# A hybrid decoder step on one core: a third staging tile, p copies in rows' tiles, reloads into settled places, and gates first in the last pair

## The chip, the cores and the metric

The kernel runs on one core of one Trainium2 chip. The metric is the device time of one execution in microseconds, as the median of several runs. Beside it there is one profiled execution, from which all rows below are taken.

## The reference

A decoder trunk with one layer of each of two mixers, run for 1024 prompt tokens and 8 sample tokens with shared weights (W = 384, 384 and 264 columns: two blocks of prompt tokens, and a third with the last 256 and the 8 samples).

```python
for i in range(2):
    hn = rmsnorm(h, norm_mix[i])
    if i == 0:   # HGRN2: q, f, i, z = split(hn @ w_in_a); 8 heads, dk 128, dv 256
        y, S = hgrn2_mixer(hn, s_hgrn[j], ...)      # S_t = diag(f_t) S_(t-1) + k_t v_t^T, o_t = S_t^T q_t
                                                    # y = (rmsnorm(o) * silu(z)) @ w_out
    else:        # gated MLP: u, v, z = split(hn @ w_in_b), u = gelu(u), v = layernorm(gelu(v))
        s = einsum('gts,bnsgd->bntgd', w_spatial, v) + b_spatial   # 8 groups, chunks of 128 tokens
        y = (u * s * silu(z)) @ w_out
    h = h + y
    gate = sigmoid(rmsnorm(h, norm_ple[i]) @ w_ple_gate[i])
    h = h + gate * (p[i] @ w_ple_proj[i])
y = rmsnorm(h, norm_final)
```

It returns the outputs for prompt and samples, the HGRN2 states of both, and the normalised v rows of the last chunk.

## The kernel before

Everything lies with features on the partitions and tokens in the columns, in the three column blocks c = 0, 1, 2. A product in full precision is three matmuls on high and low halves (`mm3`, L213 to L215: hi x hi, lo x hi, hi x lo). A weight tile is fetched into `wstg`, cast to its high half `whi` by ScalarE (L145), and VectorE subtracts that to get the low half `wlo` (L146). Activations are split the same way (L208, L209). `tc.high_priority(offset=PRI)` lets a scheduler put the instructions inside it earlier in their engine's order; otherwise they stand about as the code is written, and each engine works through its own order. SyncE issues all the transfers, in its order too.

**Heads.** Eight heads of layer 0 run one after the other, as several generators that are advanced in turns by ticks. In a head, `q` and `k` are multiplied by decay factors level by level (L644, L645), `k` is then transposed on TensorE (`pt_k`, L660). The gate path `zs` (L541) uses sigmoids in a ring of two tiles `sg`. In the last head (h = 7) the same ring also holds the p input of layer 0 (`p_in_act(0, ...)`, L334), which is fetched and split there. `out_sum` (L671, L672) copies a head's output and sums its squares.

**Units.** Layer 1's three input products are done in units of 2x2 blocks with seven products instead of eight (`unit`): weight tiles `a[0]` and `a[1]` of a unit are fetched (`load_unit`, L178), GpSimd makes sums of their quarters (`ssum`, L182 to L189), and ScalarE and VectorE split these (`shi`, `slo`) and the plain ones. In `unit`, VectorE adds the products up in `u2`, `u4` and `c22`; the sum `c` (L1121) reads the bank `ps_d`, which a later product writes again. For each group g from 0 to 7 there is a gated unit (for u, with a gelu) and then a spatial unit (for z): in it TensorE multiplies the v rows by `w_spatial` (`psp`, L1206), VectorE scales that and adds `bt` (`s`, L1208), GpSimd multiplies by u (L1214), ScalarE takes the sigmoid of z (L1219), VectorE multiplies twice (L1220, L1221), and SyncE stores the result to `ozd` (L1222). All `wstg` tiles come from one ring of two.

**The last pair.** While group 7's spatial unit runs, the stored results are fetched again for the output projection: `load_zt`/`zq` makes 20 transfers of 128x384 into a ring of five tiles `zq` (L346), each split by ScalarE (L350) and VectorE (L353). Behind the unit comes the second half of p's product, `pple(1, ph, pl, 1, ...)`: 12 groups `ps_pple`, each copied by ScalarE to `pple_t` (L329) in a ring of four tiles and stored to `ppd` (L330). `ps_pple` has three banks. Then come the products of the output projection (`ps_o`).

**Norms.** `norm_sum` adds a constant to the column sums `pss` (L268, and L270 for the block c = 2, which has 8 columns more), GpSimd takes the power -1/2 (L222), TensorE spreads it over the partitions (`pbc`, L278).

Of the kernel before, what the change touches and what calls it, by code (L numbers as in the profile page):

```python
# [7 lines left out]
F32 = mybir.dt.float32  # L8
# [71 lines left out]
def trunk_kernel(ctx, tc, xT, st, pT, nrm, wina, lbl, gna, wouta, winb, lng, lnb, lngr, lnbr,  # L80
# [59 lines left out]
    ws = [None]  # L140
# [32 lines left out]
    def load_unit(m):  # L173


        a = [wp.tile([P, 1024], F32, name="wstg") for _ in range(2)]
# [74 lines left out]
    def norm_sum(sp, ssq, c):  # L251

        nt = NT[c]
        cols = nt + (c == 2)
        pss = pp.tile([P, 512], F32, name="pss", tag="po", bufs=1)
        e = sp.tile([P, 3], F32, name="rms_e", bufs=2)
        if c == 2:
            V.memset(e, 1.0)
# [10 lines left out]
        if c == 2:  # L269
            V.tensor_scalar(e[:NS, 2:3], pss[:NS, 2:3], D * EPS, None, ALU.add)  # L270
        return rsqrt(sp, e, 3)

    def norm_bc(y, c):

        pbc = p2[0].tile([P, 512], F32, name="pbc", tag="p2", bufs=2)
        for i in range(NT[c] + (c == 2)):
            n = min(P, W[c] - i * P)
            PE.matmul(pbc[:, i * P:i * P + n], y[:n, i:i + 1].broadcast_to([n, P]), ident[:n, :n], start=True, stop=True)  # L278
# [58 lines left out]
    def load_zt(zt, parts, stage, n=2, lag=0, tie=True):  # L337
# [4 lines left out]
        for i in range(len(todo) + lag):  # L342
            if i < len(todo):
                c, k0, k = todo[i]
                stg.append(stage(W[c]))
                last["zt"] = nc.sync.dma_start(stg[i], ozd[c][:, k0 + k:k0 + k + n, :])  # L346
            if i >= lag:
# [5 lines left out]
                V.tensor_tensor(zl[:, k:k + n, :], stg[i - lag], zh[:, k:k + n, :].bitcast(F32), ALU.subtract)  # L353
            yield
# [67 lines left out]
    fill = pple(0, ph, pl, 0, [(sp, "pple_t", 9)] * 9 + [(fq, "q", 3)] * 3)  # L422
# [82 lines left out]
    def head_proj(h, r):  # L505
# [873 lines left out]
```

## Time and profile before

| | |
|---|---|
| median of 3 runs | 1933.78 us (1931.57 to 1937.53) |
| profiled execution | 1936.32 us, span of its core 1934.6 us |
| mean granted TensorE clock | 0.991 of full speed |
| TensorE busy | 1887.6 us, 13250 matmuls |
| VectorE, ScalarE, GpSimd busy | 1162.3, 800.0, 429.5 us |

A row of a timeline gives the start, the duration, the engine (PE = TensorE, DVE = VectorE, ACT = ScalarE, POOL = GpSimd, SP = SyncE; SPq is SyncE's queue), the line of the kernel, the operation, the tile written and the tiles read, and in brackets the idle time before it with what ended it. Several equal instructions in a row are one row with xN. A wait's row gives the engine and what it stood for, the sum in us, how often, and the longest. Clock shares are of 2.4 GHz; the lower level is 1.2 GHz.

### The profile page before, as it was taken

To read this page: it belongs to the slowest core of one execution; us is meant where nothing else is said; L and a number is where in the kernel's file an instruction comes from. 1 tells how busy PE (TensorE), PEld (TensorE's weight loads), DVE (VectorE), ACT (ScalarE), POOL (GpSimd) and SP (SyncE) were. 2 spreads that over 40 slices of the span, in tenths; PEclk is the share of its full clock that TensorE was granted. 3 is DMA by queue.
4 is the path that set the end of the run, shared out by engine and by line. 5 is a ranking of instruction groups with operands and counts; after the bars stand their busy time and mean duration, and the time that the engine had idled before them with its cause. 6 is when DMAs were issued, how large, how long until landed. Compare 5 with 4: busy or idle time off the path is not lost.

```text
span 1934.6 us, 33674 instructions
## 1 busy us (share of the span) xinstructions
PE 1887.6 (98%) x13250; PEld 1857.7 (96%) x13250; DVE 1162.3 (60%) x2610; ACT 800.0 (41%) x1701; POOL 429.5 (22%) x441
## 2 busy tenths in 40 slices
PE   9999999999999999999999999999999998999997
PEld 8999999999999998999999999999999997999997
DVE  5967776776767676311555655586677776311455
ACT  6453535445454536311344544433343335211242
POOL 4110001001000100011333322344444441011221
PEclk8999999999999999999999999999999999999999
DMA  6232322222231327611244333333323236611123
GB/s 211 75 117 70 110 72 96 78 80 97 72 110 51 109 71 228 215 44 44 94 138 138 98 123 97 96 105 108 96 96 100 100 109 212 191 53 44 66 88 110
DMA packets 123887, 203.75 MB, mean 105 GB/s; under 512 B 11409, under 2 KB 96593, under 8 KB 122705
## 3 DMA queue, kind: packets, MB, share of 16 engines
q1 hardware_dynamic: 123728, 201.61, 32.2%
q8 instruction: 104, 1.70, 0.4%
q14 instruction: 55, 0.44, 0.1%
HBM read 148.75 MB, written 52.82 MB: 104 GB/s over the span
## 4 chain that ended last, share of the span: by engine, by line
PE 78%; DVE 10%; DMA 4%; issue 3%; POOL 2%; ACT 2%; SPq 0%; DVEq 0%; POOLq 0%; ACTq 0%
PE ps_proj L213 15%; PE ps_proj L214 15%; PE ps_proj L215 15%; PE ps_o L213 6%; PE ps_o L214 6%; PE ps_o L215 6%; DVE wlo L146 1%; DMA vn<-vraw 1%; PE ps_d L213 1%; PE ps_d L215 1%; PE ps_d L214 1%; PE pC L642 1%; PE pt_o L683 1%; DMA wstg<-in_winb 1%; PE p L608 1%
## 5 line engine op out<-in xcount | busy, mean ns | idle before, releaser
L213 PE MATMUL ps_proj<-bh,whi 128*128 128x384 f32 (+1 forms) x2160 | 695.8, 322 | 4.0 <-DVE zs L541 2.4
L214 PE MATMUL ps_proj<-bl,whi 128*128 128x384 f32 (+1 forms) x2160 | 679.2, 314 | 1.2 <-POOL bl L209 1.2
L215 PE MATMUL ps_proj<-bh,wlo 128*128 128x384 f32 (+1 forms) x2160 | 679.9, 315 | 0.2 <-DVE wlo L146 0.2
L213 PEld LDWEIGHTS ps_proj<-bh,whi 128*128 128x128 f32 x2160 | 407.8, 189 | 5.7 <-DVE zs L541 3.0
L214 PEld LDWEIGHTS ps_proj<-bl,whi 128*128 128x128 f32 x2160 | 408.2, 189 | 2.3 <-POOL bl L209 2.3
L215 PEld LDWEIGHTS ps_proj<-bh,wlo 128*128 128x128 f32 x2160 | 406.8, 188 | 0.8 <-DVE wlo L146 0.8
L146 DVE TENSOR_TENSOR wlo<-wstg,whi 128x1024 fp32r<-128x1024 f32 x148 | 190.3, 1285 | 129.1 <-ACT whi L145 128.3
L145 ACT CAST whi<-wstg 128x1024 fp32r<-128x1024 f32 x148 | 155.2, 1049 | 129.1 <-PE ps_proj L214 72.9
L249 POOL TENSOR_TENSOR ssq<-ssq,tmp 128x384 f32<-128x384 f32 (+1 forms) x72 | 76.2, 1058 | 407.1 <-ACT tmp L248 360.3
L862 DVE TENSOR_TENSOR h<-h,ps_o 128x384 f32<-128x384 f32 (+1 forms) x48 | 24.6, 512 | 193.8 <-PE ps_o L215 188.4
L248 ACT ACTIVATE tmp<-h 128x384 f32<-128x384 f32 (+1 forms) x72 | 35.3, 491 | 219.2 <-DVE h L862 168.8
L145 ACT CAST shi<-ssum 128x512 fp32r<-128x512 f32 x88 | 53.9, 621 | 172.1 <-POOL ssum L182 97.4
L213 PE MATMUL ps_o<-bh,whi 128*128 128x384 f32 (+1 forms) x384 | 122.1, 318 | 0.0
L214 PE MATMUL ps_o<-bl,whi 128*128 128x384 f32 (+1 forms) x384 | 121.8, 317 | 0.0
L215 PE MATMUL ps_o<-bh,wlo 128*128 128x384 f32 (+1 forms) x384 | 121.8, 317 | 0.0
L146 DVE TENSOR_TENSOR slo<-ssum,shi 128x512 fp32r<-128x512 f32 x88 | 73.7, 839 | 51.5 <-ACT shi L145 51.5
L213 PE MATMUL ps_o<-zh,whi 128*128 128x384 f32 (+1 forms) x288 | 90.1, 313 | 0.0
L215 PE MATMUL ps_o<-zh,wlo 128*128 128x384 f32 (+1 forms) x288 | 89.7, 312 | 0.0
L214 PE MATMUL ps_o<-zl,whi 128*128 128x384 f32 (+1 forms) x288 | 89.7, 312 | 0.0
L209 POOL TENSOR_TENSOR ql<-q,qh 128x384 fp32r<-128x384 f32 (+1 forms) x24 | 22.7, 947 | 234.1 <-ACT qh L208 218.8
L214 PEld LDWEIGHTS ps_o<-bl,whi 128*128 128x128 f32 x384 | 72.2, 188 | 0.0
L213 PEld LDWEIGHTS ps_o<-bh,whi 128*128 128x128 f32 x384 | 72.2, 188 | 0.0
(283 smaller groups left out, 3901.3 us busy)
## 6 DMA issues: line engine op xcount, KB each, us to landing
wstg<-in_wina SPq DMA_DIRECT2D x48, 512.0 KB, 3.6
wstg<-in_winb SPq DMA_DIRECT2D x48, 512.0 KB, 4.0
zstg<-ozd SPq DMA_DIRECT2D x22, 384.0 KB, 3.9
pj<-ppd SPq DMA_DIRECT2D x16, 516.0 KB, 4.0
S<-in_st SPq DMA_DIRECT2D x16, 512.0 KB, 4.8
vb<-vd SPq DMA_DIRECT2D x16, 512.0 KB, 5.0
out_so_s<-S SPq DMA_DIRECT2D x16, 512.0 KB, 3.3
wstg<-in_wouta SPq DMA_DIRECT2D x16, 512.0 KB, 3.7
```

What stands on the lines that cost most here:

```text
L145: A.copy(hi, src)
L146: V.tensor_tensor(lo, src, hi.bitcast(F32), ALU.subtract)
L209: last["lo"] = eng.tensor_tensor(lo, src, hi.bitcast(F32), ALU.subtract)
L213: PE.matmul(ps, wh, xh, start=first, stop=False, skip_group_check=more)
L214: PE.matmul(ps, wh, xl, start=False, stop=False, skip_group_check=more)
L215: PE.matmul(ps, wl, xh, start=False, stop=last, skip_group_check=more)
L248: A.activation(sq[:, :w], src, AF.Square)
L249: eng.tensor_tensor(ssq, ssq, sq[:, :w], ALU.add)
L608: PE.matmul(blk(p0, i), blk(Y, i), blk(X, i), start=True, stop=True)
L642: PE.matmul(pC[b:b + l, o + l:o + 2 * l], kb, qb, start=True, stop=True)
L683: PE.transpose(pt[:, m, :], on[:, m * P:(m + 1) * P], ident)
L862: V.tensor_tensor(hr[c][m], hr[c][m], ps[:, :W[c]], ALU.add)
```

## The change

- **Third staging tile.** Every third allocation of `load_unit` takes a tile `wstg3` of its own, so a unit's second weight tile reuses the first one of the unit before.
- **Spatial units.** The operation `s` (L1208, now L1231) has high priority in all of them. In group 7 the sigmoid and both products have it as well.
- **Reloads.** The 20 reloads of the last pair go to five places that the last spatial unit's first operations have finished with (`rw` twice, `bspb` twice, `gb`), and each next one is fetched behind a split instead of ahead of it.
- **p copies.** The last half of p's product is copied into the 12 tiles `hr[c][4 + mm]`, which later hold rows of h, instead of a ring of four.
- **Last head.** p of layer 0 goes through the ring `vf` instead of `sg`; the decay products of q and k and the operations of `out_sum` have high priority there. In all heads, `sample` has two ticks more ahead of each update of its state and fewer behind them.
- **Norms.** All sums `pss` fill 128 rows, so one operation adds the constant for every block, and no memset is needed.

```diff
 def load_unit(m):
-    a = [wp.tile([P, 1024], F32, name="wstg") for _ in range(2)]
+    a = []
+    for _ in range(2):
+        a.append(ws[0].tile([P, 1024], F32, name="wstg3", bufs=1) if nst[0] % 3 == 2 else
+                 wp.tile([P, 1024], F32, name="wstg"))
+        nst[0] += 1
...
 def norm_sum(sp, ssq, c):
         for i in range(cols):
-            n = min(P, W[c] - i * P)
+            o = min(i * P, W[c] - P)
             for j, t in enumerate(parts):
-                PE.matmul(pss[:n, i:i + 1], t[:, i * P:i * P + n], ones[:, 0:1],
+                PE.matmul(pss[:, i:i + 1], t[:, o:o + P], ones[:, 0:1],
                           start=j == 0, stop=j == len(parts) - 1)
-        V.tensor_scalar(e[:, :nt], pss[:, :nt], D * EPS, None, ALU.add)
-        if c == 2:
-            V.tensor_scalar(e[:NS, 2:3], pss[:NS, 2:3], D * EPS, None, ALU.add)
+        e = sp.tile([P, 3], F32, name="rms_e", bufs=2)
+        V.tensor_scalar(e, pss[:, :3], D * EPS, None, ALU.add)
...
 pple:
-                pl_, tag, bufs = stg[n % len(stg)]
-                n += 1
-                t = pl_.tile([P, 384], F32, name="pple_t", tag=tag, bufs=bufs)
+                t = place(c, mm)
...
 load_zt:
+            if not lag:
+                fetch(i)
             if i >= lag:
                 ...
+            if lag:
+                fetch(i)
...
-                    r["p"] = p_in_act(0, lambda w: fq.tile([P, 384], F32, name="sg", bufs=2)[:, :w])
+                    r["p"] = p_in_act(0, lambda w: wa.tile([P, 384], F32, name="vf", bufs=2)[:, :w])
...
-            V.tensor_tensor(ql[:, :, 1, :], ql[:, :, 1, :], t2[:, :, 0:1].broadcast_to([P, n, lv]), ALU.mult)
-            V.tensor_tensor(kl[:, :, 0, :], kl[:, :, 0, :], t2[:, :, 1:2].broadcast_to([P, n, lv]), ALU.mult)
+            with tc.high_priority(offset=PRI if h == NH - 1 else 0):
+                V.tensor_tensor(ql[:, :, 1, :], ql[:, :, 1, :], t2[:, :, 0:1].broadcast_to([P, n, lv]), ALU.mult)
+                V.tensor_tensor(kl[:, :, 0, :], kl[:, :, 0, :], t2[:, :, 1:2].broadcast_to([P, n, lv]), ALU.mult)
...
 out_sum:
+        with tc.high_priority(offset=PRI if last_head[0] else 0):
...
 sample:
             nc.sync.dma_start(vb, ...)
+            yield 2
...
-        yield 10
+        yield 6
...
 spatial, pre():
+            with tc.high_priority(offset=PRI):
                 V.scalar_tensor_tensor(s[:, :nt * P]..., pss[:, :nt, :], lg[:, 0, m:m + 1], bts[mm]..., ...)
 spatial, out():
+            with tc.high_priority(offset=PRI if g == 7 else 0):
                 A.activation(sg[:, :w], src, AF.Sigmoid)
                 V.tensor_tensor(sg[:, :w], sg[:, :w], src, ALU.mult)
                 V.tensor_tensor(s[:, :w], s[:, :w], sg[:, :w], ALU.mult)
...
+            zq_to = itertools.cycle([t[:, 3 * i:3 * i + 3, :].rearrange("p a b -> p (a b)") for t in (rw, bspb)
+                                     for i in range(2)] + [gb.rearrange("p a b -> p (a b)")[:, :384]])
             zq = load_zt(zt, [(1, 0), (0, 0), (1, 4), (1, 8)],
-                         lambda w: wb2.tile([P, 384], F32, name="zq", bufs=ZQ)[:, :w].rearrange(...),
+                         lambda w: next(zq_to)[:, :w].rearrange("p (k t) -> p k t", k=1),
                          1, ZQ, False)
...
-              ..., pple(1, ph, pl, 1, [(sp, "tmp", 4)]))
+              ..., pple(1, ph, pl, 1, lambda c, mm: hr[c][4 + mm]))
```

GpSimd's order at a spatial unit and the gated unit behind it, before (L1214 are the products `s` by u, L182 and L187 the first two sums of the gated unit, L1243 and L1244 the normalised rows of the last chunk):

```order
L1214 TENSOR_TENSOR s<-s,u 128x264
L189 TENSOR_TENSOR ssum<-wstg,ssum 128x512
L1214 TENSOR_TENSOR s<-s,u 128x384 x3
L1213 COPY s<-ss__14932 128x8
L1214 TENSOR_TENSOR s<-s,u 128x264
L182 TENSOR_TENSOR ssum<-wstg 128x512
L187 TENSOR_TENSOR ssum<-wstg 128x512
L1243 TENSOR_TENSOR gb<-vn,gb 128x256
L1244 TENSOR_TENSOR gb<-gb 128x256
L184 TENSOR_TENSOR ssum<-ssum,wstg 128x512
L189 TENSOR_TENSOR ssum<-wstg,ssum 128x512
```

and of the change, where L1237 are these products and L188 and L193 these sums:

```order
L1237 TENSOR_TENSOR s<-s,u 128x384
L195 TENSOR_TENSOR ssum<-wstg,ssum 128x512
L1237 TENSOR_TENSOR s<-s,u 128x384
L188 TENSOR_TENSOR ssum<-wstg 128x512
L193 TENSOR_TENSOR ssum<-wstg 128x512
L1237 TENSOR_TENSOR s<-s,u 128x384
L1236 COPY s<-ss__14926 128x8
L1237 TENSOR_TENSOR s<-s,u 128x264
L190 TENSOR_TENSOR ssum<-ssum,wstg 128x512
L1267 TENSOR_TENSOR gb<-vn,gb 128x256
L1268 TENSOR_TENSOR gb<-gb 128x256
L195 TENSOR_TENSOR ssum<-wstg,ssum 128x512
```

The two sums that stood behind the last product `s` now stand ahead of the last two products of the spatial unit.

ScalarE's order at the end of the last spatial unit, before (L1219 the sigmoids, L350 the casts of reloads, L329 the copies of p's product):

```order
L350 CAST xmh_11627<-zq 128x384
L145 CAST whi<-wstg 128x1024
L350 CAST xmh_11627<-zq 128x384 x2
L1219 ACTIVATE sg<-u_18599 128x384
L350 CAST xmh_11627<-zq 128x384
L329 COPY pple_t<-ps_pple 128x384 x3
L350 CAST zh_0_18852<-zstg 128x528
L329 COPY pple_t<-ps_pple 128x384
L350 CAST zh_0_18852<-zstg 128x528
```

and of the change (L1243 the sigmoids, L363 the casts, L338 the copies):

```order
L363 CAST xmh_11621<-bspb 128x384
L146 CAST whi<-wstg 128x1024
L1243 ACTIVATE sg<-u_18588 128x384
L363 CAST xmh_11621<-rw 128x384
L363 CAST xmh_11625<-rw 128x384
L363 CAST xmh_11625<-bspb 128x384 x2
L363 CAST xmh_11625<-gb 128x384
L338 COPY h_4_18786<-ps_pple 128x384
L338 COPY h_5_18787<-ps_pple 128x384
L338 COPY h_6_18788<-ps_pple 128x384
L363 CAST zh_0_18826<-zstg 128x528
L338 COPY h_7_18789<-ps_pple 128x384
```

Five casts of reloads now stand between the last sigmoid and the first copy, where one stood. VectorE's order at the same place, of the change (L1155 the last sum of the unit, L1244 and L1245 the products behind a sigmoid, L366 the low halves of reloads):

```order
L366 TENSOR_TENSOR bl_11636<-rw,bh_11633 128x384
L1245 TENSOR_TENSOR s<-s,sg 128x384
L1155 TENSOR_TENSOR u_18588<-ps_d,u_18588 128x384
L366 TENSOR_TENSOR xml_11622<-bspb,xmh_11621 128x384 x2
L1244 TENSOR_TENSOR sg<-sg,u_18588 128x384
L366 TENSOR_TENSOR xml_11622<-gb,xmh_11621 128x384
L1245 TENSOR_TENSOR s<-s,sg 128x384
L366 TENSOR_TENSOR xml_11622<-rw,xmh_11621 128x384
L366 TENSOR_TENSOR xml_11626<-rw,xmh_11625 128x384
L147 TENSOR_TENSOR wlo<-wstg,whi 128x1024
L366 TENSOR_TENSOR xml_11626<-bspb,xmh_11625 128x384 x2
L366 TENSOR_TENSOR xml_11626<-gb,xmh_11625 128x384
```

The low half of the reload in `gb` now stands behind the product of the last sigmoid, and the low halves of the last five reloads behind that.

VectorE's order in the last head, before (L644 and L645 the decay products, L541 the gate path `zs`, L146 the low half of a weight tile):

```order
L541 SCALAR_TENSOR_TENSOR zs_9299<-ps_proj,gn_707,sg 128x384
L209 TENSOR_TENSOR Sl<-S,Sh 128x256
L209 TENSOR_TENSOR bl_125<-sg,bh_122 128x264
L353 TENSOR_TENSOR bl_123<-zstg,bh_120 128x768
L644 TENSOR_TENSOR q<-q,t_9557 128x2x64
L146 TENSOR_TENSOR wlo<-wstg,whi 128x1024
L645 TENSOR_TENSOR k<-k,t_9557 128x2x64
L650 TENSOR_TENSOR asum<-Am_712,pC 128x256
L541 SCALAR_TENSOR_TENSOR zs_9300<-ps_proj,gn_707,sg 128x384
L708 SCALAR_TENSOR_TENSOR S<-S,t_9427,pd 128x256
L209 TENSOR_TENSOR al<-asum,ah 128x256
```

and of the change (L661 and L662 the decay products, L557 `zs`, L147 the low half):

```order
L366 TENSOR_TENSOR bl_123<-zstg,bh_120 128x768
L557 SCALAR_TENSOR_TENSOR zs_9297<-ps_proj,gn_705,sg 128x384
L661 TENSOR_TENSOR q<-q,t_9546 128x2x64
L662 TENSOR_TENSOR k<-k,t_9546 128x2x64
L728 SCALAR_TENSOR_TENSOR S<-S,t_9405,pd 128x256
L667 TENSOR_TENSOR asum<-Am_710,pC 128x256
L366 TENSOR_TENSOR bl_123<-zstg,bh_120 128x768
L215 TENSOR_TENSOR Sl<-S,Sh 128x256
L366 TENSOR_TENSOR bl_123<-zstg,bh_120 128x768
L147 TENSOR_TENSOR wlo<-wstg,whi 128x1024
L215 TENSOR_TENSOR al<-asum,ah 128x256
```

The product for `k` stood behind the low half `wlo`; now it and `q` stand ahead of it, and `al` stands behind it.

## Rows read from the trace of the kernel before

**Rows 1.** the page's busy time, share of the span and instructions of each engine

```profile
PE 1887.6 (98%) x13250; PEld 1857.7 (96%) x13250; DVE 1162.3 (60%) x2610; ACT 800.0 (41%) x1701; POOL 429.5 (22%) x441
```

**Rows 2.** TensorE's waits, whole span: us in total, times, longest us

```profile
PE ps_d L213 <- DVE c L1121: 8.6, 7, 2.4
PE ps_pple L213 <- ACT pple_t L329: 7.9, 4, 5.4
PE pt_k L660 <- DVE k L645: 3.1, 1, 3.1
PE ps_proj L213 <- DVE zs L541: 2.4, 2, 1.7
PE psp L1206 <- DVE s L1208: 1.2, 1, 1.2
```

**Rows 3.** windows: length, busy us (instructions) of each engine, granted clock, DMA share, GB/s

```profile
745.00:755.00 10.00, 8.00 (x53) 7.17 (x54) 8.03 (x14) 6.85 (x18) 1.87 (x2) 0.83 0.59 176
1310.00:1320.00 10.00, 7.61 (x41) 7.29 (x40) 4.67 (x7) 3.33 (x6) 3.68 (x4) 0.83 0.30 92
1360.00:1370.00 10.00, 8.08 (x46) 8.07 (x46) 4.43 (x7) 4.62 (x8) 1.90 (x3) 0.83 0.30 81
1637.50:1645.00 7.50, 7.41 (x38) 7.41 (x39) 3.17 (x4) 5.60 (x12) 0.00 (x0) 0.70 0.96 329
```

**Rows 4.** all engines' waits in the units, 1255 to 1600 us

```profile
POOL ssum L182 <- DMA wstg<-in_winb: 102.8, 12, 11.3
DVE slo L146 <- ACT shi L145: 29.7, 16, 2.9
```

**Rows 5.** timeline of SyncE and VectorE about one gated unit: start us, us, instruction

```profile
1336.61 0.33 SPq L178 DMA_DIRECT2D wstg<-in_winb  x1
1347.97 0.33 SPq L178 DMA_DIRECT2D wstg<-in_winb  x1
...
1360.72 0.69 DVE L146 TENSOR_TENSOR slo<-ssum,shi 128x512 fp32r<-128x512 f32 x1 [2.06 <-ACT shi L145]
1361.33 0.55 DVE L1121 TENSOR_TENSOR c<-ps_d,u 128x384 f32<-128x384 f32 x1
```

**Rows 6.** timeline of VectorE and GpSimd in the spatial unit before it

```profile
1328.33 1.11 DVE L146 TENSOR_TENSOR slo<-ssum,shi 128x512 fp32r<-128x512 f32 x1 [2.27 <-ACT shi L145]
1340.31 0.68 DVE L146 TENSOR_TENSOR slo<-ssum,shi 128x512 fp32r<-128x512 f32 x1
1345.65 0.56 DVE L1221 TENSOR_TENSOR s<-s,sg 128x384 f32<-128x384 f32 x1
...
1341.59 1.26 POOL L1214 TENSOR_TENSOR s<-s,u 128x384 f32<-128x384 f32 x1 [2.29 <-DVE s L1208]
```

**Rows 7.** DMA issues in the units: KB each, median us from issue to landing

```profile
wstg<-in_winb SPq DMA_DIRECT2D x28, 512.0 KB, 3.7
zq<-ozd SPq DMA_DIRECT2D x5, 192.0 KB, 3.3
```

**Rows 8.** timeline of TensorE, ScalarE and VectorE at the last pair

```profile
1626.46 0.45 PE L213 MATMUL ps_pple<-bh,whi 128*128 128x384 f32 x1 [1.27 <-ACT pple_t L329]
1637.59 0.69 PE L213 MATMUL ps_pple<-bh,whi 128*128 128x384 f32 x1 [5.38 <-ACT pple_t L329]
1643.50 0.28 PE L215 MATMUL ps_pple<-bh,wlo 128*128 128x264 f32 x1
...
1625.54 0.49 ACT L350 CAST xmh<-zq 128x384 fp32r<-128x384 f32 x1
1637.06 0.48 ACT L329 COPY pple_t<-ps_pple 128x384 f32<-128x384 f32 x1 [5.67 <-DMA ppd<-pple_t]
...
1623.70 0.55 DVE L1133 TENSOR_TENSOR u<-ps_d,u 128x384 f32<-128x384 f32 x1
```

**Rows 9.** timeline of ScalarE and VectorE in the last head

```profile
738.81 0.83 ACT L208 CAST bh<-sg 128x384 fp32r<-128x384 f32 x2 [2.89 <-DMA sg<-in_pT]
...
746.13 0.82 DVE L645 TENSOR_TENSOR k<-k,t 128x128 f32<-128x128 f32 x1
```

More of the change, by code (lines that the diff above doesn't have):

```diff
@@ L251, in norm_sum @@
     def norm_sum(sp, ssq, c):
-        nt = NT[c]
-        cols = nt + (c == 2)
+        cols = NT[c] + (c == 2)
         pss = pp.tile([P, 512], F32, name="pss", tag="po", bufs=1)
-        e = sp.tile([P, 3], F32, name="rms_e", bufs=2)
-        if c == 2:
-            V.memset(e, 1.0)
         parts = ssq if isinstance(ssq, list) else [ssq]
@@ L277, in norm_bc @@
             n = min(P, W[c] - i * P)
-            PE.matmul(pbc[:, i * P:i * P + n], y[:n, i:i + 1].broadcast_to([n, P]), ident[:n, :n], start=True, stop=True)
+            PE.matmul(pbc[:, i * P:i * P + n], y[:, i:i + 1].broadcast_to([P, P]), ident[:, P - n:], start=True, stop=True)
         return pbc
@@ L313, in load_p, with places, place, pple @@
         V.tensor_tensor(pl[c], stg, ph[c].bitcast(F32), ALU.subtract)
-    def pple(l, ph, pl, half, stg):
+    def places(stg):
+        n = [0]
+        def place(c, mm):
+            pl_, tag, bufs = stg[n[0] % len(stg)]
+            n[0] += 1
+            return pl_.tile([P, 384], F32, name="pple_t", tag=tag, bufs=bufs)[:, :W[c]]
+        return place
+    def pple(l, ph, pl, half, place):
         wh, wl = take("p", l, half)
-        n = 0
         for c in CH:
@@ L341, in load_zt, with fetch @@
         stg = []
-        for i in range(len(todo) + lag):
+        def fetch(i):
             if i < len(todo):
@@ L346, in load_zt @@
                 last["zt"] = nc.sync.dma_start(stg[i], ozd[c][:, k0 + k:k0 + k + n, :])
+        for i in range(len(todo) + lag):
+            if not lag:
+                fetch(i)
             if i >= lag:
@@ L421, in trunk_kernel @@
     V.tensor_scalar(g32, g32, 32.0, None, ALU.mult)
-    fill = pple(0, ph, pl, 0, [(sp, "pple_t", 9)] * 9 + [(fq, "q", 3)] * 3)
+    fill = pple(0, ph, pl, 0, places([(sp, "pple_t", 9)] * 9 + [(fq, "q", 3)] * 3))
     def first_norm(c):
@@ L799, in last_fill @@
     def last_fill():
-        yield from pple(0, ph, pl, 1, [(wa, t, 2 if t == "vf" else 1) for t in ("vf", "E", "R", "vf", "X", "Y")])
+        yield from pple(0, ph, pl, 1, places([(wa, t, 2 if t == "vf" else 1) for t in ("vf", "E", "R", "vf", "X", "Y")]))
         run(load_zt(zt, [(2, 0)], stage2(wa, 2), tie=False))
@@ L982, in trunk_kernel @@
             ple(0, ep, act[0], act[1], ssq2, lambda c: tk.spawn(norm_rows(c, ssq2, 2, hn, NDEL[1][c])), mid)
-            for i, _ in enumerate(pple(1, ph, pl, 0, [(pq, "pple_t", 8)])):
+            for i, _ in enumerate(pple(1, ph, pl, 0, places([(pq, "pple_t", 8)]))):
                 if i % 2:
@@ L1142, in trunk_kernel @@
     mv = wb.tile([P, 8, 2], F32, name="mv")
-    ss_ = wb.tile([P, MI, NS], F32, name="ss_")
+    ss_ = wb2.tile([P, MI, NS], F32, name="ss_")
     ln = {}
@@ L1151, in layer_norm @@
         ln["rstd"] = rsqrt(wb, ve, 8)
[L1154 to L1155 removed]
+        sv = wb2.tile([P, MI, NS], F32, name="sv")
+        sx = wb2.tile([P, MI, NS], F32, name="sx")
         s1 = wb.tile([P, NS], F32, name="s1")
```

33 lines of the change are left out of this document (16 added, 17 removed).

## Prediction

> **What bounds the kernel now.** First the busy shares: TensorE has work in 98% of the span, no other engine in more than 60% [rows 1]. So only two things can be won: the 2% in which TensorE stands, and the stretches in which its clock is low. Next I read what TensorE waited for, longest first [rows 2]. 8.6 us in seven waits are for `c`, the VectorE sum inside a unit; 7.9 us in four are for ScalarE's copies of p's product (`pple_t`); 3.1 us in one wait is for `k` in the last head; `zs` has two waits, 2.4 with the longest 1.7, and the shorter one, 0.7, lies just ahead of that wait for `k`; `psp` has one of 1.2. Third, the granted clock around the long ones [rows 3]: 0.83 over the 10 us that begin at the head's wait and at the two long waits for `c` (2.4 us is the longest), and 0.70 over the 7.5 us after the wait for the copies. The missing share times the length is time lost: 1.7 us three times, and 2.2 us once. Behind a removed wait such a loss goes too.
>
> Then who is late. In the units GpSimd's first sum waited 102.8 us in twelve waits for the transfer of the second weight tile, and VectorE's `slo` waited 29.7 us for ScalarE, which stands behind those sums [rows 4]. `c` stands behind such a `slo` in VectorE's order. One unit shows it [rows 5]: SyncE issued the unit's first weight tile at 1336.61 and its second at 1347.97, because that one reuses a tile that is freed only after the end of the unit before; `slo` then stood idle 2.06 us until 1360.72, and `c` came at 1361.33. Between them lies a delay of 11.4 us that no transfer needs.
>
> **The third staging tile.** It adds no instruction. The second weight tile goes into a tile freed in the middle of the unit before, so its issue can move ahead by up to those 11.4 us, and the sums on GpSimd, the casts and `slo` follow. The largest `slo` idle that stands ahead of `c` is 2.06 us here, well under what is moved. I take 8.0 of the 8.6 us; 0.6 is left as an estimate, since `c` itself (0.55 us in [rows 5]) starts when TensorE's product ends and can't be hidden entirely. The low clock behind the two long waits goes with them, 2 x 1.7 = 3.4. Bounds: 0, if something else holds `c`, and 8.6 + 3.4 = 12.0.
> What it costs: GpSimd's first two sums of a gated unit now stand ahead of the spatial unit's last two products `s`. In [rows 6] such a product began at 1341.59 and took 1.26 us; the second tile would land 3.7 us after an issue at 1336.6, as these transfers do [rows 7], the two sums take about 1.3 us each, so the product begins near 1342.9 instead and ends at 1344.1. VectorE used it at 1345.65. So 1.5 us of cover hides it and I cost it at nothing; without the cover VectorE would stand there, with the sigmoid's products and the next unit's `u` behind it.
> On contention the rows speak against the change. A `slo` of 128x512 that ran while GpSimd worked took 1.11 us (1328.33); one that began with GpSimd idle took 0.68 (1340.31) [rows 6]. The moved sums now run beside VectorE's products. At 0.43 us for each sum and seven units that is 7 x 2 x 0.43 = 6.0 us of VectorE time. TensorE waits for VectorE in the spatial units in no wait but `psp`'s 1.2, so I take nothing, and keep 6.0 as a bound.
> The Trainium skill, "SBUF — State Buffer", section "Who interferes with whom", states that a VectorE instruction with two SBUF inputs contends with a GpSimd instruction that reads SBUF. The two durations of `slo` agree with it. By that rule the sum would be the same where VectorE has slack, and 6.0 us worse where it has none.
>
> **The last pair (spatial unit 7 and p's product behind it).** The early `s` takes `psp`'s wait of 1.2. The p copies go to 12 tiles of their own, so no copy waits any more for a store: the copy at 1637.06 had stood 5.67 us for one, and TensorE with it, 5.38 us until 1637.59 [rows 8]. From 1625.2, when TensorE first stood (1.27 us before 1626.46), to its last p matmul at 1643.6 are 18.4 us; 7.7 of them were waits (three of the four) and 2.2 low clock, so 8.5 us were work.
> But the order moves something else: five reload casts (`rw`, `rw`, `bspb`, `bspb`, `gb`) now stand behind the last sigmoid and ahead of the first copy; before, one did, at 1625.54, and the copies began right after it. The last reload can be issued only when VectorE has taken the low half out of the reload before it in `gb`, and that half stands behind `u`, two halves and a product. `u` ran at 1623.70 before [rows 8], behind a reload half and an `s` that now stand elsewhere; I put it at 1623.0. `u`, the two halves, the product and the half take 0.55 + 1.0 + 0.55 + 0.55, to about 1625.6. A reload lands 3.3 us after its issue [rows 7], so this one at about 1628.9; its cast takes 0.5, the first copy 0.5: TensorE goes on at 1629.9, after standing from 1625.2 - 1.2 = 1624.0. With 8.5 us of work and 2.2 us of low clock again it ends at 1640.6: 3.0 us won, `psp` included. If the reloads run as in the profile (last cast 1625.54), TensorE goes on at 1626.5 and loses 1.7 in clock: 1636.7, 6.9 won. With no wait at all: 1632.5, 11.1 won. If the chain is 3 us slower still, 0. I take 3.0, since the five casts are in the order as it stands.
> The gates first and the places of the reloads have no price beyond this: both move the same instructions. Reloads into `rw`, `bspb` and `gb` need these free, which the last spatial unit's first operations settle.
>
> **The last head.** ScalarE's cast of p stood 2.89 us for a transfer into the tile `sg` that the sigmoids use too, and `k` ran at 746.13 behind `wlo` [rows 9]. Now p has the ring `vf`, and the decay products go ahead of `wlo`. The waits for `k` and `zs` are 3.1 + 0.7, the clock behind them 1.7: 5.5. Late next is `al`, now behind `wlo` and two low halves; I leave 1.0 for it, an estimate from one such operation, and take 4.5. Bounds 0 and 5.5. The later update of the sample state moves work that TensorE does not wait for.
>
> **The norms.** One short VectorE operation less, and a memset, in each norm of the last column block. No row of these prices it; VectorE's sums over 384 columns take 0.55 us [rows 5], these have 3 columns, so 0 to 0.55 for each norm that TensorE waits for. I take 0.2 in all, near the lower end.
>
> **Sum.** 8.0 + 3.4 + 3.0 + 4.5 + 0.2 = 19.1 us. The profiled execution took 1936.3 us (span 1934.6 and 1.7 around it), so 1917.2 for it. It lies 2.5 us over the median of 1933.8; measured from that, 1914.7.
>
> **Rivals.** All times are from the median.
> - The pair gives back more: the reloads are as quick as before or quicker, 6.9 to 11.1 instead of 3.0. Then 1906.6 to 1910.8. For it: ScalarE and VectorE have less ahead of the sigmoids. Against it: the row of five casts. 0.16.
> - The third tile gives half: `slo` is held by GpSimd's order instead, where the two `gb` products stand between the sums. 5.7 us less: 1920.4. 0.14. Here belongs contention as well: VectorE without slack, 6.0 us worse, 1920.7, by the chance that the waits for `u` or `s` become TensorE's: 0.07. The skill's rule named above would give the same 1920.7.
> - The units gain alone, pair and head put a new wait where the old one was (11.6 us): 1922.2. 0.08.
> - The change does not do what it says: the tile is free no earlier, or SyncE stands at stores ahead of the issue, so little but the head's 4.5 comes: 1929. 0.05.
> - Slower: GpSimd, standing at the early sum until the transfer lands, holds the product `s`, VectorE stands for it, and the three `s` tiles fill, so TensorE stands at `psp`. Each us beyond the 1.5 us of cover is lost in seven units. It decides from 19.1 / 7 = 2.7 us beyond the cover, a landing 4.2 us later than worked out; 1 us more gives 1940. The slot at 1341.59 and SyncE's issue of the first tile on time speak against. 0.03.
>
> **Numbers.** The forecast itself has 0.47: 1915 us, with 1911 to 1919 as its own range. The range of all cases is 1906 to 1925: it takes in the pair's and the units' bounds and leaves out the last two cases and the far ends. About 0.3% (5.8 us) is what a measurement of this kernel can tell from no change. Faster by more than that: 0.88; within: 0.08 (the case in which it does little, and part of the gains that a new wait eats); slower: 0.04.
>
> **What would show it.** Right: no wait of TensorE for `c` over 0.5 us and a clock of 1 through the units; GpSimd's wait for weight transfers in the units far under 102.8; no wait for `k` in the last head; in the pair one wait for a p copy of about 6 us in place of three, with the clock low behind it, and ScalarE's copies starting some 4 us after its last sigmoid. Wrong: if VectorE's `s` products wait for GpSimd, if waits at `psp` or `u` in the spatial units appear, if the copies start within 2 us of the last sigmoid (then the time is nearer 1908), or if a wait for zstg reloads or `al` stands where the removed waits were.

## The result and the profile after

The change takes 1919.85 us (median of 6 runs, 1918.46 to 1921.93) where the kernel before takes 1933.39 (6 runs, 1931.06 to 1937.53): a ratio of 0.9927, interval 0.9913 to 0.9942. The forecast was 1915, with 1911 to 1919 as its own range and 1906 to 1925 as the range of all cases, so the time lies 0.85 us above the first and inside the second. The profiled execution took 1921.39 us (span 1919.7).

First the busy shares, from the page, which answer to [rows 1]:

```profile
PE 1883.1 (98%) x13250; PEld 1856.4 (97%) x13250; DVE 1156.6 (60%) x2600; ACT 799.9 (42%) x1701; POOL 433.4 (23%) x441
```

No share tells that 15 us went. TensorE's waits over the whole span do, and they answer to [rows 2]:

```profile
PE ps_pple L219 <- ACT h L338: 8.6, 1, 8.6
PE po L219 <- ACT pos L692: 2.7, 1, 2.7
...
PE pos L793 <- ACT po L692: 1.9, 1, 1.9
```

The waits for `c`, `k`, `zs` and `psp` are gone. The four for the copies of p's product are one, and it is longer than they were together (8.6 against 7.9). Those for `pos` and `po` are new. GpSimd's waits in the units, 1255 to 1600 us, answer to [rows 4]:

```profile
POOL s L1237 <- DVE s L1231: 59.6, 24, 7.2
...
POOL ssum L188 <- DMA wstg<-in_winb: 51.2, 13, 6.3
```

The wait for weight transfers halved (102.8 before), and GpSimd stands longer for VectorE's `s` instead; TensorE has no wait behind that. SyncE, GpSimd and VectorE of the change at the gated unit that [rows 5] showed, and then GpSimd of the kernel before at the same first sum:

```profile
1332.39 0.33 SPq L184 DMA_DIRECT2D wstg<-in_winb  x1
1336.05 1.58 POOL L188 TENSOR_TENSOR ssum<-wstg 128x512 f32<-128x512 f32 x1 [1.26 <-DMA wstg<-in_winb]
...
1352.08 0.76 DVE L147 TENSOR_TENSOR slo<-ssum,shi 128x512 fp32r<-128x512 f32 x1
1353.00 0.56 DVE L1143 TENSOR_TENSOR c<-ps_d,u 128x384 f32<-128x384 f32 x1 [0.16 <-PE ps_d L221]
```

```profile
1353.42 1.29 POOL L182 TENSOR_TENSOR ssum<-wstg 128x512 f32<-128x512 f32 x1 [8.29 <-DMA wstg<-in_winb]
```

The transfer at 1332.39 is the unit's second weight tile, and the first sum begins as it lands. It is issued 20.6 us ahead of `c` where that was 13.4 (1347.97 to 1361.33 in [rows 5]): 7.2 us earlier against the unit's own work, of the 11.4 that the prediction gave as the most, and the first sum waits 1.26 us where it waited 8.29. The low half `slo` no longer stands for ScalarE, and `c` stands for TensorE, where before TensorE stood for `c`. The head's window of [rows 3] and the one behind it, all units in one window, and the last pair at its long wait, with the granted clock as the third number from the end and the DMA share behind it:

```profile
745.00:755.00 10.00, 5.46 (x44) 4.35 (x43) 8.05 (x14) 7.29 (x18) 1.76 (x1) 1.00 0.80 225
755.00:765.00 10.00, 10.00 (x58) 9.83 (x56) 4.05 (x9) 7.09 (x20) 1.25 (x2) 0.83 0.70 237
1255.00:1605.00 350.00, 348.92 (x2330) 348.34 (x2329) 261.15 (x417) 143.25 (x232) 165.94 (x139) 1.00 0.33 108
1610.00:1615.00 5.00, 0.00 (x0) 0.00 (x0) 4.85 (x9) 1.54 (x3) 0.00 (x0) 0.72 0.94 282
```

The units run at the full clock. In the last head TensorE has work in 5.46 of 10 us, where it had 8.00, and the low clock has not gone but moved: 0.83 in the ten us behind that window, where the kernel before had 1.00.

**Where the time went.** The table gives lengths in us between the starts of named matmuls in each kernel's timeline: from the start of the span to the last head's first `pt_k`; from there to the first `ps_o` (the head); the step between the second and third `pbc` of layer 0's gate phase (norm); from that `pbc` to group 7's first `psp` (units); from there to the first of the last twelve `ps_pple` (last group); and from there to the next `ps_o` (p's product). Names of kernels are those of the experiments below.

```
                 to head   head  norm   units  last group  p's product
before            710.98  58.21 10.77  530.61     25.50       21.73
after             711.17  58.70  9.21  517.01     24.05       22.16
e1_no_third       707.45  57.46  9.21  542.41     24.05       23.45
e2_head_undone    715.26  56.46  9.18  516.63     24.05       21.64
e3_norm           708.63  56.94  9.21  529.93     25.22       21.87
e4_row_tiles      709.09  59.38 10.75  529.75     25.87       21.79
e7_ticks          713.08  56.98  9.21  520.20     24.05       22.16
e8_no_gates       708.71  57.67  9.21  518.31     24.05       20.88
e9_s_late         711.32  58.07  9.22  515.68     24.06       22.64
e10_neither       708.91  56.93  9.22  527.96     24.06       21.70
e11_late4         711.28  58.04  9.21  517.40     24.06       17.50
e12_both          709.50  56.45  9.18  516.27     24.06       17.40
e13_both_head     709.73  58.00  9.18  516.37     24.05       17.25
e14_half_tiles    712.94  55.06  9.19  516.31     24.06       17.72
```

Before less after: units 13.6, last group 1.45, p's product -0.4, head -0.5, norm 1.6; with -0.8 from the other stretches, for which nothing was forecast (-0.2 up to the head, -0.2 between head and norm, -0.4 behind p's product), these are the 14.9 us between the two spans. Each length is that of one execution. The stretch up to the last head differs by up to 8 us between kernels in which no edit but the norms' and sample's ticks falls there, so an edit of 2 us is read from its own stretch.

### The profile page after: what moved, and what is told of

Its sections match the earlier page's. It is cut to its first block, busy times and chain, and to the rows that moved or that the text cites. A ratio compares the mean times of both kernels' runs of the same rounds, so it can differ in the third digit from the quotient of the medians.

```text
span 1919.7 us, 33670 instructions
## 1 busy us (share of the span) xinstructions
PE 1883.1 (98%) x13250; PEld 1856.4 (97%) x13250; DVE 1156.6 (60%) x2600; ACT 799.9 (42%) x1701; POOL 433.4 (23%) x441
## 4 chain that ended last, share of the span: by engine, by line
PE 90%; DVE 5%; DMA 3%; ACT 1%; issue 1%; POOL 1%; SPq 0%; DVEq 0%; ACTq 0%; POOLq 0%
PE ps_proj L219 18%; PE ps_proj L221 18%; PE ps_proj L220 18%; PE ps_o L219 6%; PE ps_o L220 6%; PE ps_o L221 6%; PE ps_d L221 2%; PE ps_d L219 2%; PE ps_d L220 2%; PE psp L1228 1%; PE pt_o L703 1%; PE pC L658 1%; PE pss L269 1%; PE p L624 1%; DMA vb<-vd 1%
## 5 line engine op out<-in xcount | busy, mean ns | idle before, releaser
L147 DVE TENSOR_TENSOR wlo<-wstg,whi 128x1024 fp32r<-128x1024 f32 x148 | 186.2, 1258 | 140.6 <-ACT whi L146 139.8
L146 ACT CAST whi<-wstg 128x1024 fp32r<-128x1024 f32 x148 | 155.1, 1048 | 160.2 <-PE ps_proj L220 105.8
L146 ACT CAST shi<-ssum 128x512 fp32r<-128x512 f32 x88 | 54.6, 621 | 109.1 <-PE ps_proj L220 59.2
L147 DVE TENSOR_TENSOR slo<-ssum,shi 128x512 fp32r<-128x512 f32 x88 | 68.9, 784 | 11.9 <-ACT shi L146 11.9
L661 DVE TENSOR_TENSOR q<-q,t 128x192 f32<-128x192 f32 (+1 forms) x144 | 47.1, 328 | 45.1 <-PE pC L658 38.7
```

Of the source, the lines that this page charges most:

```text
L146: A.copy(hi, src)
L147: V.tensor_tensor(lo, src, hi.bitcast(F32), ALU.subtract)
L661: V.tensor_tensor(ql[:, :, 1, :], ql[:, :, 1, :], t2[:, :, 0:1].broadcast_to([P, n, lv]), ALU.mult)
```

## Experiments

The kernel before ran beside them in three groups: 1934.48 us (e1 to e4), 1936.87 (e7, e9, e10, e11) and 1935.11 (e8, e12, e13, e14). Each ratio is to the group's own.

**The third tile left out.** All else as in the change.

```diff
-            a.append(ws[0].tile([P, 1024], F32, name="wstg3", bufs=1) if nst[0] % 3 == 2 else
-                     wp.tile([P, 1024], F32, name="wstg"))
+            a.append(wp.tile([P, 1024], F32, name="wstg"))
```

> The change with its third staging tile taken out again (two ring tiles, as before), all else kept. Theory: the landmarks of the two traces move by 13.5 us across the units, so this run should lose 12 to 14 us against the change: about 1933, with 8 to 9 us of TensorE's waits for c back and the low clock behind the two longest. Rival 1, the size in the prediction: 11.4 us, about 1931. Rival 2: the high priority of the operation s did part of it, since it took slo out of VectorE's way; then less than 9 us are lost, 1929 or below, and the waits for c stay under 5 us.

Measured: 1944.06 us (1935.67 to 1953.86), ratio 1.0048 [1.0030, 1.0066], slower than the kernel before. TensorE waits 15.7 us for `c` in seven waits, 3.5 the longest, and the units take 25.4 us more than in the change. That is more than any of the three cases said, so something else in the change costs some 10 us when this tile is missing.

**Which other part costs it: the early `s`.** One kernel puts `s` back to its old place in groups 0 to 6, with the third tile; the other does so without it.

```diff
-            with tc.high_priority(offset=PRI):
+            with tc.high_priority(offset=PRI if g == 7 else 0):
                 V.scalar_tensor_tensor(s[:, :nt * P]...
```

> The change with the operation s at its old place in groups 0 to 6 (no high priority there; third tile kept). Theory 1, the third tile carries the units and the early s only costs where c is late already: no wait for c, units within 2 us of the change, 1918 to 1922 us. Theory 2, the two add up (the run without the third tile lost some 10 us in the units against the kernel before, so the early s would cost that here too): about 10 us faster than the change, 1908 to 1912. Theory 3, both are needed together, since the late s holds the gated unit's sums on GpSimd behind it: waits for c come back, 1925 to 1933.

> The change without the third tile and without the early s of groups 0 to 6. Theory 1, the units lost 10 us against the kernel before in the run without the third tile because of the early s: waits for c fall from 15.7 back to about 8.6 us and the time to that of the kernel before less 2 us for the norms and the pair, 1930 to 1934. Rival: the loss came from another part (reloads into settled places, sample's ticks), and it stays: waits for c of 14 us or more, 1940 to 1945.

Measured: e9 1917.51 us (1916.64 to 1920.00), ratio 0.9903 [0.9886, 0.9919]; e10 1927.65 (1927.20 to 1930.76), 0.9960 [0.9945, 0.9975], waits for `c` 7.6. In both the mechanism of the first theory held, while the times lie 0.5 and 2.4 us below the ranges that it gave. By the stage lengths the third tile is worth 12.3 us (527.96 less 515.68) where `s` is late and 25.4 where it is early; the early `s` costs 14.5 us without the tile and 1.3 with it (over all kernels with the tile, 517.9 in the mean of five with the early `s` and 516.2 in that of four without).

The same place in both shows how: TensorE, GpSimd, VectorE and SyncE of e1_no_third, in the timeline,

```profile
1325.78 0.42 PE L218 MATMUL ps_d<-xmh,shi 128*128 128x384 f32 x1
...
1327.68 1.39 POOL L1236 TENSOR_TENSOR s<-s,u 128x384 f32<-128x384 f32 x1 [2.49 <-DVE s L1230]
...
1328.12 1.24 DVE L1244 TENSOR_TENSOR s<-s,sg 128x264 f32<-128x264 f32 x1
...
1339.77 1.22 DVE L147 TENSOR_TENSOR wlo<-wstg,whi 128x1024 fp32r<-128x1024 f32 x1
...
1341.33 0.37 SPq L183 DMA_DIRECT2D wstg<-in_winb  x1
...
1355.92 0.69 PE L218 MATMUL ps_d<-bh,whi 128*128 128x384 f32 x1 [3.50 <-DVE c L1142]
```

and of e10_neither:

```profile
1325.75 0.42 PE L218 MATMUL ps_d<-xmh,shi 128*128 128x384 f32 x1
...
1327.69 1.42 POOL L194 TENSOR_TENSOR ssum<-wstg,ssum 128x512 f32<-128x512 f32 x1 [2.57 <-DVE slo L147]
...
1327.54 0.42 DVE L1244 TENSOR_TENSOR s<-s,sg 128x264 f32<-128x264 f32 x1
...
1338.64 1.22 DVE L147 TENSOR_TENSOR wlo<-wstg,whi 128x1024 fp32r<-128x1024 f32 x1
...
1340.14 0.37 SPq L183 DMA_DIRECT2D wstg<-in_winb  x1
...
1354.19 0.44 PE L218 MATMUL ps_d<-bh,whi 128*128 128x384 f32 x1 [1.81 <-DVE c L1142]
```

TensorE is at the same place (1325.8) in both, and GpSimd starts an instruction at 1327.7 in both. With the early `s` ahead of it in VectorE's order, VectorE's `s<-s,sg` begins 0.44 us behind that start and takes 1.24 us; without, it begins 0.15 us ahead of it and takes 0.42. The longer one ends 0.3 us after the GpSimd product (1329.36 and 1329.07). VectorE is 1.1 us later at `wlo`, the second weight tile is issued 1.2 us later, and TensorE stands 1.7 us longer, with slow matmuls behind (0.69 us the first). Over the units SyncE's issues of weight tiles stand 45.1 us for `wlo` in six waits here and 39.3 in e10; at this place the issue stands behind a store, which waits for VectorE's product too, and two reloads. In seven units that is 8.1 us more of TensorE's waits (15.7 less 7.6); the rest is the lower clock of e1, here first, and then e10:

```profile
1255.00:1605.00 350.00, 334.10 (x2166) 331.57 (x2165) 253.00 (x381) 129.21 (x205) 156.38 (x134) 0.98 0.30 99
```

```profile
1255.00:1605.00 350.00, 342.36 (x2261) 340.05 (x2262) 255.08 (x403) 139.27 (x226) 160.24 (x136) 1.00 0.32 105
```

The difference is about 7 us by these rounded shares. The Trainium skill, "SBUF — State Buffer", section "Who interferes with whom", states that a VectorE instruction with two SBUF inputs contends with a GpSimd instruction that reads SBUF. The prolonged instruction has two and ran beside such a one, so its 1.24 us agree.

**The last head as before.** p back in `sg`, decay products, `out_sum` and ticks at their old places.

```diff
-  ... wa.tile([P, 384], F32, name="vf", bufs=2)
+  ... fq.tile([P, 384], F32, name="sg", bufs=2)
-  with tc.high_priority(offset=PRI if h == NH - 1 else 0):
+  with tc.high_priority(offset=0):
-  with tc.high_priority(offset=PRI if last_head[0] else 0):
+  with tc.high_priority(offset=0):
-            yield 2
-        yield 6
+        yield 10
```

> The change with everything in the heads as before (p through the ring sg, no priority for the decay products and out_sum, sample's ticks as before). Theory: the change's three parts in the last head removed 4.3 us of waits and put 4.8 us of new ones behind them, so undoing them changes nothing: 1919 to 1921, with the waits for k and zs back and those for the copies of po and pos gone. Rival, the prediction's term: 4.5 us worse, 1924 to 1925.

Measured: 1921.98 us (1918.73 to 1922.63), ratio 0.9929 [0.9912, 0.9945], the time of the change: 1 us above the theory's range and 2 below the rival's. The waits for `k` and `zs` are back, those for `pos` and `po` gone. Only sample's ticks undone:

```diff
-            yield 2
-        yield 6
+        yield 10
```

> The change with the ticks of sample as before (the update of the sample state not put off). Theory 1, in the last head the reloads into zstg come late because SyncE stands at the store of the sample state, which waits for that update: they start 3 us or more earlier against TensorE's place, the casts on ScalarE no longer hold the copies of out_sum, the waits for pos and po (4.7 us together) go, 1915 to 1917 us. Rival, the reloads and the early out_sum itself are late for their own reason: waits stay, 1919 to 1921.

Measured: 1920.00 us (1916.58 to 1925.24), ratio 0.9920 [0.9900, 0.9939]. The waits for `pos` and `po` are 3.4 us in place of 4.6, not gone, and the time is the rival's: the first theory fell. But TensorE has a wait back that lies far from the last head, from 60 to 120 us:

```profile
PE ps_proj L219 <- DVE zs L557: 1.7, 1, 1.7
```

It stands in all six kernels without the ticks (1.4 to 2.4 us) and in none of the eight with them, so the ticks remove it; the prediction gave them nothing. It is the longer of the two waits for `zs` in [rows 2]. What it brings in time can't be told from the stretch up to the last head. ScalarE and TensorE in the last head of the change show what holds them:

```profile
747.38 0.83 ACT L363 CAST bh<-zstg 128x768 fp32r<-128x768 f32 x1 [0.84 <-DMA zstg<-ozd]
748.12 0.36 ACT L691 COPY on<-po 128x256 f32<-128x256 f32 x1
...
753.21 0.51 ACT L745 ACTIVATE on<-on,rsq 128x256 f32<-128x256 f32 x1 [1.61 <-POOL rsq L228]
753.62 0.35 ACT L691 COPY on<-pos 128x256 f32<-128x256 f32 x1
...
748.93 1.07 PE L793 MATMUL pos<-S,qm 128*32 128x256 f32 x16 [1.89 <-ACT po L692]
754.41 0.39 PE L219 MATMUL po<-vh,ah 128*128 128x256 f32 x1 [2.65 <-ACT pos L692]
```

A cast of a `zstg` reload stands ahead of the copy of `po`, and waits for its transfer; the scaling that waits for GpSimd's `rsq` stands ahead of that of `pos`. The early `k` brings TensorE here 4 us sooner, but not the reloads: the cast at 747.38 comes 36.2 us after the head's start (711.17), and the same one of the kernel before, at 746.00, 35.0 us after it (710.98).

**One operation for the norms, alone on the kernel before.**

```diff
-        V.tensor_scalar(e[:, :nt], pss[:, :nt], D * EPS, None, ALU.add)
-        if c == 2:
-            V.tensor_scalar(e[:NS, 2:3], pss[:NS, 2:3], D * EPS, None, ALU.add)
+        V.tensor_scalar(e, pss[:, :3], D * EPS, None, ALU.add)
```

> The kernel before with the one operation for the norms' constant alone. Theory: in one norm of the last column block the second operation stood 2.4 us behind the first in VectorE's order, and TensorE waited 1.6 us for it; so 1.5 us faster than before, near 1932, with the waits for pbc at 2.2 us instead of 3.8. Rival, the prediction's term: 0.2 us, no visible change of those waits.

Measured: 1933.28 us, ratio 0.9997 [0.9986, 1.0007]. The time does not tell it from no change; in its own stretch 10.77 falls to 9.21, and to 9.18 to 9.22 in all others with the edit. VectorE, GpSimd and TensorE of the kernel before, and then VectorE and GpSimd of the change, at the third norm of layer 0's gate phase:

```profile
1060.91 0.15 DVE L268 TENSOR_SCALAR rms_e<-pss 128x2 f32<-128x2 f32 x1
...
1063.28 0.14 DVE L270 TENSOR_SCALAR rms_e<-pss 8x1 f32<-8x1 f32 x1
...
1063.58 2.15 POOL L222 TENSOR_TENSOR rsq<-rms_e,mhalf 128x3 f32<-128x3 f32 x1 [1.69 <-DVE rms_e L270]
...
1065.78 1.02 PE L278 MATMUL pbc<-ident,rsq 128*128 128x128 f32 x6 [1.59 <-POOL rsq L222]
```

```profile
1061.77 0.15 DVE L272 TENSOR_SCALAR rms_e<-pss 128x3 f32<-128x3 f32 x1
...
1062.90 0.85 POOL L228 TENSOR_TENSOR rsq<-rms_e,mhalf 128x3 f32<-128x3 f32 x1
```

The second operation takes 0.14 us, but stood 2.4 us behind the first in VectorE's order; GpSimd's power, which waited for it, also took 2.15 us at that place and 0.85 in the change. TensorE's wait of 1.59 us behind it is gone in the change.

**p copies in the rows' tiles, alone on the kernel before.**

```diff
-              ..., pple(1, ph, pl, 1, places([(sp, "tmp", 4)])))
+              ..., pple(1, ph, pl, 1, lambda c, mm: hr[c][4 + mm]))
```

> The kernel before with the last p copies in rows' tiles alone (the reloads in their ring of five as before, one reload cast behind the last sigmoid). Theory 1: the waits for stores go, 6.4 us with the low clock behind the longest, and nothing comes in their place, because only one cast stands ahead of the copies: 5 to 8 us faster than before, 1926 to 1928. Then the five casts that the reloads' new order puts ahead of the copies are what took this gain away. Theory 2: the copies find another wait (rows' tiles that are free only after the last product of the sigmoid, at about 1631): 0 to 3 us, 1930 to 1933.

Measured: 1934.71 us, ratio 1.0002 [0.9988, 1.0016]. ScalarE's copy behind the long wait, in its timeline:

```profile
1635.08 0.48 ACT L336 COPY h<-ps_pple 128x384 f32<-128x384 f32 x1 [5.45 <-DMA ozd<-s]
```

The rows' tiles lie where other tiles were. In place of the store of an earlier copy (5.67 us in [rows 8]) this one waits for the store of a late `s` (waits 6.9 against 7.9). The time is that of the second theory. That the edit gains once `s` is earlier is a reading of this row: no run has the two alone.

**The last pair's gates at their old places.** Only the sigmoid and both products of group 7; its `s` stays early.

```diff
-            with tc.high_priority(offset=PRI if g == 7 else 0):
+            with tc.high_priority(offset=0):
```

> The change with the sigmoid and the two products of group 7 at their old places. Theory 1, the gates' place brings nothing by itself, since the copies of p stand behind the reloads' casts either way: one wait for the copies of 8 to 9 us, 1919 to 1921 us. Rival, the later gates push the last s and its store and the low halves of the reloads back, so the wait for the copies grows by 2 us or more: 1922 to 1925.

Measured: 1916.92 us (1914.40 to 1918.45), ratio 0.9904 [0.9889, 0.9918]; p's product takes 20.88 us against 22.16. Neither theory: in this stretch the gates first cost 1.3 us, while the intervals of e8 and of the change overlap. ScalarE's order with them late, in the timeline:

```profile
1610.11 0.51 ACT L363 CAST xmh<-gb 128x384 fp32r<-128x384 f32 x1 [0.77 <-DMA gb<-ozd]
...
1610.99 0.52 ACT L1243 ACTIVATE sg<-u 128x384 f32<-128x384 f32 x1
1612.93 1.24 ACT L338 COPY h<-ps_pple 128x384 f32<-128x384 f32 x3 [1.41 <-DVE sg L1244]
```

All casts stand ahead of the last sigmoid, and the copies follow it in 1.9 us.

**The last four reloads taken late.** Their rows are needed only in the second half of a product of the output projection.

```diff
-            zq = load_zt(zt, [(1, 0), (0, 0), (1, 4), (1, 8)],
+            zq = load_zt(zt, [(1, 0), (0, 0), (1, 4)],
-              ... [(2, 0), (0, 8), (1, 12), (2, 8)], pple(...
+              ... [(2, 0), (0, 8), (1, 8), (1, 12), (2, 8)], pple(...
```

> The change with the last four reloads of the last pair (the rows 8 to 11 of the second block) taken through the later zstg reloads, so one cast in place of five stands between the last sigmoid and the first p copy. Theory 1, the five casts with their reloads hold the copies: the copies start about 2.5 us after the last sigmoid, the one wait of 8.6 us falls to 3 to 4 us, 1914 to 1916 us. Rival, the transfers are the limit there (DMA share 0.83): the same bytes come later and ps_o stands for them, total waits from 1605 to 1700 us stay at 8 us or more, 1918 to 1921.

Measured: 1914.11 us (1912.35 to 1916.56), ratio 0.9888 [0.9873, 0.9902]. The first theory held; ScalarE and TensorE in its timeline:

```profile
1609.64 0.52 ACT L1243 ACTIVATE sg<-u 128x384 f32<-128x384 f32 x1 [0.59 <-DVE u L1155]
1612.08 0.51 ACT L363 CAST xmh<-rw 128x384 fp32r<-128x384 f32 x1 [1.91 <-DMA rw<-ozd]
1612.49 1.23 ACT L338 COPY h<-ps_pple 128x384 f32<-128x384 f32 x3
...
1613.02 0.45 PE L219 MATMUL ps_pple<-bh,whi 128*128 128x384 f32 x1 [3.79 <-ACT h L338]
```

One cast stands between, the wait is 3.8 in place of 8.6, p's product takes 17.50 us, and no wait over 0.3 us for `ps_o` appears later. Its interval lies apart from that of the change.

**Versions put together.** e12 joins e11 and e9. e13 undoes the last head in it, as in e2. e14 takes e12 and reloads in the last heads through four tiles of one block column:

```diff
-  load_zt(zt, [(c, 0)], stage2(wa, 2), tie=False)
+  load_zt(zt, [(c, 0)], lambda w: wa.tile([P, 1, 384], F32, name="zstg", bufs=4)[:, :, :w], 1, tie=False)
```

> The change with the last four reloads of the last pair taken late (as in e11_late4) and s at its old place in groups 0 to 6 (as in e9_s_late). Theory 1, the two act in different stretches and add: 4.7 us of the last pair and 1.3 us of the units by the traces, some 6 us under the change, a ratio of 0.986 to 0.988. Rival, the units' part was chance (its interval overlapped with that of the change): the time of e11_late4, 0.9885 or more.

> e12_both with all edits of the last head and of sample's ticks undone. Theory 1, in the last head the reloads into a ring of two zstg tiles set the pace, so what the early decay products win is stood again at the copies of out_sum: as fast as e12_both or up to 2 us faster (the trace with the head undone came 2.2 us earlier out of the head than the change), the waits for pos and po gone and those for k (3.1) and zs back. Rival, the early products bring what was forecast (4.5): 3 to 5 us slower than e12_both.

> e12_both with the reloads of the last heads in four tiles of one column of blocks in place of two tiles of two: the same bytes and space, twice the transfers, casts and low halves, each half as long. Theory 1, the ring of two sets the pace in the last head, so shorter pieces get through it sooner: the waits of TensorE for pos and po (4.4 us) fall under 2, 2 to 5 us faster than e12_both. Rival, SyncE and the transfers set it, or the casts stand in ScalarE's order ahead of the copies anyway: waits of 4 us or more, the time of e12_both or slower.

Measured: e12 1912.74 us (1911.28 to 1914.22), ratio 0.9883 [0.9868, 0.9898]; e13 1916.72 (1914.46 to 1917.79), 0.9902 [0.9887, 0.9917]; e14 1909.29 (1908.42 to 1914.32), 0.9864 [0.9847, 0.9880]. By the stages e12's two parts add (p's product 17.40, units 516.27), though its interval cannot tell it from e11 alone. e13 is 4.0 us slower than e12 by the medians, which is the rival's size, though the intervals overlap; its head is 1.55 us longer. e14 has the shortest head of all (55.06); its waits there are:

```profile
PE pos L793 <- ACT po L692: 1.5, 1, 1.5
PE po L219 <- ACT pos L692: 1.1, 1, 1.1
```

That is 2.6 together, against 2.8 in e12 and 4.6 in the change: not under 2 as its theory asked, and its interval overlaps that of e12. Whether shorter pieces help stays open. e14 is faster than the change itself, with intervals apart.

## Why the prediction held, and where its terms were off

The time fell inside the range, and the largest term, the third tile, came as worked out. That the sum came as near is in part luck, since other terms missed in both directions. The time is nearest to the rivals of 1920.4 and 1920.7, but not for their reasons: the tile gave its whole term, and the head and the pair gave less.

**The third tile.** Right as a mechanism: no wait for `c`, full clock. The term was 11.4 us; the tile alone measured 12.3. The stage gained 13.6, since the rest of the change took another 2.65 off the units (530.61 to 527.96 in e10) and the early `s` gave 1.3 back. The traces say where the 2.65 lie: the waits for `c` are 1.0 shorter in e10 (7.6), and the clock falls once there (0.83 in 1350 to 1360) and not twice as in [rows 3], 1.7 less. Which part of the change did that is open; 0.9 of the 2.65 is within what the stage differs between the kernel before and e4.

**Cost of the early `s`: nothing.** That step was off. The prediction gave the early `s` of groups 0 to 6 no price. Its bound of 6.0 was for the sums that move on GpSimd, and it took nothing of it, because TensorE waits for VectorE in no wait of the spatial units but that for `psp`. But the second weight tile's issue waits for VectorE's `wlo`, so VectorE did have someone behind it: 14.5 us without the third tile. In the change the same product `s<-s,sg` takes 1.24 us too (at 1329.97), yet the chain has slack there, and 1.3 to 1.7 are left.

**The last pair.** Forecast 3.0, `psp`'s 1.2 in it; measured 1.0 (1.45 and -0.4). The order of the argument held: one wait behind five casts, then 10.2 us to `ps_o` (1618.08 to 1628.3) where 10.7 were worked out. What was mis-sized is the wait, 8.6 in place of 5.9. ScalarE and SyncE at the last casts of the change:

```profile
1610.35 0.52 ACT L1243 ACTIVATE sg<-u 128x384 f32<-128x384 f32 x1 [0.53 <-DVE u L1155]
...
1615.45 1.03 ACT L363 CAST xmh<-bspb 128x384 fp32r<-128x384 f32 x2 [2.31 <-DMA bspb<-ozd]
1617.14 0.51 ACT L363 CAST xmh<-gb 128x384 fp32r<-128x384 f32 x1 [0.66 <-DMA gb<-ozd]
1617.56 1.23 ACT L338 COPY h<-ps_pple 128x384 f32<-128x384 f32 x3
...
1612.25 0.42 SPq L355 DMA_DIRECT2D gb<-ozd  x1
```

The forecast put the last issue at 1625.6 in the times of before, which is 1611.3 here (14.3 earlier, the shift at group 7); it came 0.95 later. And its transfer took 4.9 us to the cast, not 3.3: [rows 7] were read in the units, where the DMA share was 0.30 [rows 3], and here it is 0.94 (1610 to 1615). The kernel before had shown such a case at this stage, with a share of 0.87 (1615 to 1620), in its issue at 1617.02:

```profile
zq<-ozd SPq DMA_DIRECT2D x1, 192.0 KB, 4.0
```

In e11, with fewer reloads, the share is 0.47 in 1610 to 1615, and its two `rw` reloads issued from 1600 to 1625 have a median of 2.8 us to landing. That the load is the cause is an argument from these cases. The copies start 7.2 us after the last sigmoid, not 4. That the gates first "have no price beyond this" was wrong too: in e8 the casts fit ahead of the sigmoid, and the stretch is 1.3 us shorter.

**The last head.** Forecast 4.5, measured -0.5 in the change. The failing step is "Late next is `al`, now behind `wlo` and two low halves; I leave 1.0 for it". The wait for `k` went as said (`pt_k` comes 4.3 us sooner against the head's start, in every kernel with the edit), but next late were ScalarE's copies of `po` and `pos`, behind casts of `zstg` reloads and a scaling, 4.6 us, with the clock's 1.7 behind them as before. The forecast had followed VectorE's queue alone, and named waits for `zstg` reloads as a sign of being wrong. Over seven kernels with the edits the head takes 56.45 to 58.70 us, mean 57.6; over five without, 56.46 to 59.38, mean 57.8. So by the stage lengths it brings about nothing. The medians of e12 and e13 differ by 4.0 us in its favour with intervals that overlap, and those of the change and e2 by none to speak of (0.9927 and 0.9929), so what it is worth stays open between the two.

**The norms.** Forecast 0.2, measured 1.56. The price was taken as the operation's own duration; what cost was its place in VectorE's order, and the GpSimd power behind it.

The sum came near because a term 2.2 too small, one 1.4 too small, and terms 5.0 and 2.0 too large stood together, and 0.8 was lost in stretches for which nothing was forecast: 19.1 forecast, 14.9 measured between the profiled executions' spans.

## What to carry to other kernels

Before a wait is counted as won, follow every queue that the waiting instruction's successors stand in, and not only that of the engine that was late: the next late one stood on ScalarE in the head and in the transfers in the last pair. An engine that TensorE does not wait for in a stage can still free the buffer that the next transfer is waiting for; ask that before its contention is priced at nothing. And read a transfer's duration in the stretch where it will run.

## What was not expected of the hardware

A VectorE product of 128x264 took 0.42 us where it began 0.15 us ahead of a GpSimd instruction, and 1.24 where it began 0.44 us behind the start of one, ending 0.3 us after it. A reload of 192 KB took 3.3 us from issue to landing in the units (median, DMA share 0.30), and 4.9 from issue to the cast that waited for it at a share of 0.94. The first 711 us took between 707.5 and 715.3 us, most of it set before 120 us; the cause is open.
